# A diffusion layer with a mixture of experts: the order of the work between the router and the first expert

## The chip, the cores and the metric

The kernel runs on one core of one Trainium2 chip. The metric is the device time of one execution in microseconds (us); three runs before gave 1791.06, 1791.74 and 1792.96, median 1791.74. A core has the matrix engine (TensorE, PE in the profile; PEld is its loading of stationary operands), VectorE (DVE), ScalarE (ACT), GpSimd (POOL) and SyncE (SP), which issues most DMAs. Each engine works its own queue in order; semaphores tie the queues together.

## The reference

One layer over 512 latent tokens of width 1024, with 256 context tokens beside them, all in 32-bit floats. First comes a mixer: modulation, a combined projection, a bidirectional state-space scan and a pooling branch, and an output projection. After it come the residual and the part that the change touches, a mixture of 32 experts of which each token takes 4:

```python
x = x + g1 * mixer_out(...)
h = modulate(rmsnorm(x, norm2_w), sh2, sc2)
logits = h @ router_w + router_b
top_val, top_idx = lax.top_k(logits, 4); gates = softmax(top_val)
# for each expert e, over the tokens that chose it:
hb  = h[toks] @ w1[e] + b1[e]              # 1024 -> 2048
g   = minimum(hb[..., ::2], 7); u = clip(hb[..., 1::2], -7, 7)
y   = (g * sigmoid(1.702 * g) * (u + 1)) @ w2[e] + b2[e]     # 1024 -> 1024
out[toks] += gate * y
x = rmsnorm(x + g2 * out, final_norm_w)
```

All 32 experts are computed, so all their weights, 12 MiB for each expert, are read once.

## The kernel before

The program is written for a framework with a planner: the source gives the instructions and their data dependences, the planner simulates the engines and writes each engine's queue in the order in which its simulation starts them. `after(i, j, NoSync)` is an edge that only fixes an order within one engine; `tc.issue_after(j)` gives such an edge to every instruction in its block that runs on j's engine. Instructions that the planner finds ready early can be queued far ahead of their place in the source.

Matrix products keep 32-bit precision by parts: a weight piece of 128 x 2048 (1 MiB, `raw`) is rounded by ScalarE to `hi` (L1093), VectorE takes the remainder `lo = raw - hi` (L1094), and each product is the sum of hi x xh, hi x xl and lo x xh (`prod`, L1353), where xh and xl are the parts of the token rows. An expert has 8 pieces of w1 and 4 of w2. There are three hi/lo pairs, and 9 raw buffers, to which two more (`pm`) are added at the start of `moe`; they lie where the router's small tiles (`pd`) lay. SP loads a piece as soon as its buffer is free (`ring_load`, L1081).

The tokens are four chunks c of 128. For chunk pairs (0, 1) and (2, 3) the output projection ends, then for each chunk `route` (square and norm, eight transposes into `h2t`, the scores by `rw` at L915, top 4, mask), `normed` (the modulated rows `h2`, stored to `h2_scr`, and the residual stored to `acc_scr`) and `table` follow. `table` ranks the tokens of each expert by a product with a triangular matrix (L968) and makes `hot0`, a 0/1 matrix that places the tokens of expert 0. `picked(j, c)` (L1004) multiplies `h2` by it: the token rows of expert 0 are gathered by TensorE, half j of the width in PSUM bank `rows0_[j]`, summed over the chunks. Before, chunks 0, 1 and 2 are picked in `table(2)` and chunk 3 in `table(3)`. `slots` fills the table of tokens and gates for the other experts.

`lead_in` is the turn. It rounds and subtracts the first three weight pieces, and between them in the source stand `in_parts` (the picked rows to xh by ScalarE, L1161, and xl by VectorE, L1162), the gather of the rows of expert 1 from `h2_scr`, and `slots` of chunks 2 and 3. `first` is the last hot matrix of chunk 3 (L977): the first `lo` comes after it on VectorE, and the later loads and the last two stores to `acc_scr` wait for it.

`moe` goes through the experts: w1 of expert p, then w2 of expert p - 1. Expert 16 has two blocks of rows. Two planning steps hang in the product loop: `order()` behind the fourth piece of expert 0 (the order of the remaining experts by their counts) and `beyond()` behind the fourth piece of expert 1 (what exceeds the planned capacities). Both use `Arena` scratch in buffers of the pool `phx`: `order` in `ah`, which before held the residual rows of chunk 3 (x13), and `beyond` in the two `y` buffers (x10 and x11, over which `normed` wrote the `h2` of chunks 2 and 3). The buffer `al` held `sh2`, one of the modulation rows.

Of the kernel before, what the change touches and what calls it, by code (L numbers as in the profile page):

```python
# [16 lines left out]
P = 128  # L17
D = 1024
KT = D // P
# [78 lines left out]
def mixer_and_moe(tc, a):  # L98
# [797 lines left out]
    tops = {}  # L896

    def route(c):
# [15 lines left out]
        for k in range(KT):  # L914
            PE.matmul(lg[:, 0:E], lhsT=h2t[:, k, :], rhs=rw[:, k, :], start=(k == 0), stop=(k == KT - 1))  # L915
# [48 lines left out]
    def table(c):  # L964
# [3 lines left out]
        PE.matmul(rk[:, 0:E], lhsT=c_("up"), rhs=mask[:, c, :], start=(c == 0), stop=True)  # L968
# [15 lines left out]
        if c == 2:  # L984
            rows0_.extend(bank("A") for _ in range(2))
            for j in range(2):
                picked(j, 0)
                picked(j, 1)
                picked(j, 2)
            return  # L990
# [10 lines left out]
    def picked(j, c):  # L1001
        for i in range(4):
            k = 4 * j + i
            PE.matmul(rows0_[j][:, i * P:(i + 1) * P], lhsT=h2s[c][:, k * P:(k + 1) * P], rhs=hot0[c],  # L1004
                      start=(c == 0 and i == 0), stop=(c == NT - 1), skip_group_check=True)
# [56 lines left out]
    newest_lo = [None]  # L1062
# [25 lines left out]
    def ring_split(r):  # L1088
        pool, th, tl, n = hring[turn[1] % len(hring)]
        hi = pool.tile([P, W], F32R, name="hi", tag=th, bufs=n)  # L1090
        lo = pool.tile([P, W], F32R, name="lo", tag=tl, bufs=n)
        turn[1] += 1
        ia = SC.activation(hi, r, AF.Copy)  # L1093
        i = VE.tensor_tensor(lo, r, hi.bitcast(F32), op=ALU.subtract)  # L1094
        newest_lo[0] = i
        if 0 < loads[0] <= LEAD:
            after(ia, last_act[0], mybir.DependencyClass.NoSync, "after the router")
            after(i, first[0], mybir.DependencyClass.NoSync, "after the first slots")
        return hi, lo
# [55 lines left out]
    def in_parts(banks):  # L1155
        hi = pc.tile([P, KT, P], F32R, name="xh", tag="xh", bufs=1)
        lo = pc.tile([P, KT, P], F32R, name="xl", tag="xl", bufs=1)
        for h, bk in enumerate(banks):
            o = hi[:, h * 4:(h + 1) * 4, :]
            v = bk.rearrange("p (k t) -> p k t", k=4)  # L1160
            SC.activation(o, v, AF.Copy)  # L1161
            i = VE.tensor_tensor(lo[:, h * 4:(h + 1) * 4, :], v, o.bitcast(F32), op=ALU.subtract)  # L1162
        return (hi, lo), i
# [8 lines left out]
    def lead_in():  # L1172
        first_ = None
        for i in range(LEAD):
            lead.append(ring_split(ring_load(w1_piece(0, i))))
            if first_ is not None:
                after(newest_lo[0], first_, mybir.DependencyClass.NoSync, "by turns")
            if i == 1:
                after(newest_lo[0], xl_, mybir.DependencyClass.NoSync, "the first rows go ahead")
            if i == 0:  # L1180
                parts0, xl_ = in_parts(rows0_)
# [13 lines left out]
    for pr in range(2):  # L1195
# [7 lines left out]
        for c in cs_:  # L1203
# [6 lines left out]
              lead, slt, sel2)  # L1210
# [45 lines left out]
def moe(tc, a, c_, cst, psa, psb, phx, pc, pd, g2, b1h, b2h, msum, top4, tab, last, table_out, acc_scr, halfneg,  # L1256
        ring, raw, load, split, w1_piece, w1_pair, w2_pair, gather_, transposed_, xgs, lead, slt, sel2):
# [158 lines left out]
    class Arena:  # L1416

        def __init__(self, tags=(("ah", 1), ("al", 1))):
# [154 lines left out]
    for p in range(E):  # L1573
        e = ids[p] = expert(p)
        m = CAPS[p][0]
        if p != MID:
# [3 lines left out]
            for k in range(KT):  # L1580
# [14 lines left out]
                if p == 1 and k == BEYOND_AT:  # L1595
                    beyond()
# [214 lines left out]
```

## Time and profile before

| what | value |
|---|---|
| median of three runs | 1791.74 us (1791.06 to 1792.96) |
| the profiled execution | 1794.53 us, span 1792.7 us |
| mean granted TensorE clock | 0.966 |
| busy share of the span | PE 92%, DVE 85%, ACT 65%, POOL 33% |
| DMA | 521 MB, 291 GB/s over the span |

The span runs from the first to the last instruction; the execution's own time is 1.8 us more. Output projection and router end at about 585 us, expert 0 begins at 590.77 us, and the experts go on until about 1770 us. In timelines a row has start, duration, engine, line, operation, what it writes and reads, shapes, and how many instructions are merged (xN); a 32-bit matrix product stands as two records. In brackets stands the time for which the engine sat idle before the row, and what ended it. A clock of 1.00 is 2.4 GHz, 0.50 is 1.2 GHz.

### The profile page before, as it was taken

To read this page: it belongs to the slowest core of one execution; us is meant where nothing else is said; L and a number is where in the kernel's file an instruction comes from. 1 tells how busy PE (TensorE), PEld (TensorE's weight loads), DVE (VectorE), ACT (ScalarE), POOL (GpSimd) and SP (SyncE) were. 2 spreads that over 40 slices of the span, in tenths; PEclk is the share of its full clock that TensorE was granted. 3 is DMA by queue.
4 is the path that set the end of the run, shared out by engine and by line. 5 is a ranking of instruction groups with operands and counts; after the bars stand their busy time and mean duration, and the time that the engine had idled before them with its cause. 6 is when DMAs were issued, how large, how long until landed. Compare 5 with 4: busy or idle time off the path is not lost. (4 is left out here: it accounts for less than half of the span.)

```text
span 1792.7 us, 21257 instructions
## 1 busy us (share of the span) xinstructions
PE 1640.6 (92%) x7311; PEld 1203.0 (67%) x7311; DVE 1526.3 (85%) x1486; ACT 1170.2 (65%) x1207; POOL 596.2 (33%) x287
## 2 busy tenths in 40 slices
PE   6999889998899899999999999999999998999985
PEld 2777667776778677767766667766666666666653
DVE  7768888987777899899999999976799999999993
ACT  6445436556643577687777777755678787777772
POOL 1203456779210011152041440502063362322302
PEclk9989999999999899999999999999999999999996
DMA  9646443223568789999999999976899999999952
GB/s 352 198 126 214 152 153 114 92 83 113 194 221 325 290 329 365 377 380 382 377 370 379 377 381 390 353 298 202 339 370 388 388 365 372 384 373 377 382 207 103
DMA packets 138417, 521.44 MB, mean 291 GB/s; under 512 B 14798, under 2 KB 44942, under 8 KB 106560
## 3 DMA queue, kind: packets, MB, share of 16 engines
q1 hardware_dynamic: 125446, 490.39, 72.1%
q0 software_dynamic: 6736, 16.70, 4.0%
q10 hardware_dynamic: 6122, 12.94, 2.2%
q8 instruction: 59, 0.97, 0.2%
q14 instruction: 54, 0.44, 0.1%
HBM read 508.26 MB, written 18.37 MB: 294 GB/s over the span
## 5 line engine op out<-in xcount | busy, mean ns | idle before, releaser
L1094 DVE TENSOR_TENSOR lo<-raw,hi 128x2048 fp32r<-128x2048 f32 x398 | 896.9, 2283 | 88.8 <-ACT hi L1093 86.2
L1093 ACT ACTIVATE hi<-raw 128x2048 fp32r<-128x2048 f32 x398 | 751.8, 1915 | 183.8 <-PE A L1353 112.8
L1376 POOL DMA_INDIRECT acc_scr<-y,ixi x32 | 220.7, 6896 | 549.4 <-DVE y L1374 445.3
L1353 PE MATMUL A<-lo,xh 128*128 128x512 f32 (+3 forms) x1072 | 314.0, 410 | 32.6 <-DVE lo L1094 28.7
L1353 PE MATMUL A<-hi,xh 128*128 128x512 f32 (+3 forms) x1072 | 308.5, 404 | 11.5 <-ACT hi L1093 6.9
L1353 PEld LDWEIGHTS A<-lo,xh 128*128 128x128 f32 (+3 forms) x1072 | 187.1, 183 | 120.7 <-DVE lo L1094 72.1
L1353 PEld LDWEIGHTS A<-hi,xh 128*128 128x128 f32 (+3 forms) x1072 | 193.9, 184 | 69.7 <-ACT hi L1093 9.6
L1117 POOL DMA_INDIRECT xg<-h_scr,ixi x30 | 114.3, 3810 | 259.6 <-PE S L1127 175.3
L1353 PE MATMUL S<-lo,ah 128*128 128x512 f32 (+3 forms) x512 | 165.3, 404 | 15.2 <-DVE lo L1094 15.1
L1353 PE MATMUL S<-hi,ah 128*128 128x512 f32 (+3 forms) x512 | 164.6, 402 | 3.9 <-DVE ah L1130 3.9
L1353 PE MATMUL A<-hi,xl 128*128 128x512 f32 (+3 forms) x544 | 155.7, 399 | 0.0
L1353 PEld LDWEIGHTS S<-lo,ah 128*128 128x128 f32 (+3 forms) x512 | 90.3, 183 | 49.9 <-DVE lo L1094 24.3
L1353 PEld LDWEIGHTS A<-hi,xl 128*128 128x128 f32 (+3 forms) x544 | 96.0, 177 | 32.1
L1353 PEld LDWEIGHTS S<-hi,ah 128*128 128x128 f32 (+3 forms) x512 | 92.5, 184 | 33.8 <-DVE ah L1130 4.0
L228 ACT ACTIVATE hi<-raw 128x1024 fp32r<-128x1024 f32 (+1 forms) x73 | 75.9, 1045 | 38.8 <-PE A L355 13.4
L231 DVE TENSOR_TENSOR lo<-raw,hi 128x1024 fp32r<-128x1024 f32 (+1 forms) x59 | 77.1, 1311 | 17.7 <-ACT hi L228 17.0
L1353 PE MATMUL S<-hi,al 128*128 128x512 f32 (+3 forms) x272 | 85.6, 396 | 0.0
L630 ACT ACTIVATE row<-row,nb 128x128 f32<-128x128 f32 x192 | 59.5, 390 | 37.4 <-POOL row L626 37.4
L336 PE MATMUL A<-hx,hi 128*128 128x512 f32 x160 | 66.5, 416 | 3.5 <-DVE at L378 2.1
L338 PE MATMUL A<-hx,lo 128*128 128x512 f32 x160 | 66.4, 415 | 0.0
L337 PE MATMUL A<-hx,hi 128*128 128x512 f32 x160 | 65.6, 410 | 0.0
L378 DVE SCALAR_TENSOR_TENSOR at<-A,cw,at 128x510 f32<-128x510 f32 (+1 forms) x80 | 57.9, 740 | 7.2 <-ACT at L374 6.6
(464 smaller groups left out, 2457.9 us busy)
## 6 DMA issues: line engine op xcount, KB each, us to landing
raw<-in_w_dram SPq DMA_DIRECT2D x384, 1024.0 KB
raw<-in_w_in_dram SPq DMA_DIRECT2D x36, 512.0 KB
mraw<-in_w_mod_dram SPq DMA_DIRECT2D x32, 512.0 KB
raw<-in_w_out_dram SPq DMA_DIRECT2D x14, 1024.0 KB
row<-cs_scr ACTq DMA_DIRECT2D x32, 384.0 KB
raw<-in_w_mod_dram SPq DMA_DIRECT2D x16, 512.0 KB
raw<-in_w_in_dram SPq DMA_DIRECT2D x16, 384.0 KB
xt<-in_x_dram SPq DMA_DIRECT2D x4, 512.0 KB
```

The source lines that it names most:

```text
L228: SC.activation(hi, r, AF.Copy)
L231: e.tensor_tensor(lo, r, hi.bitcast(F32), op=ALU.subtract)
L336: PE.matmul(lat, lhsT=hi[:, k, :], rhs=row_of(hxh, k), start=(k == 0), stop=False)
L337: PE.matmul(lat, lhsT=hi[:, k, :], rhs=row_of(hxl, k), start=False, stop=False)
L338: newest[0] = PE.matmul(lat, lhsT=lo[:, k, :], rhs=row_of(hxh, k), start=False, stop=(k == KT - 1))
L378: VE.scalar_tensor_tensor(ac[:, u:v], src[:, u + o:v + o], cw[:, j, ct:ct + 1], ac[:, u:v], op0=ALU.mult, op1=ALU.add)
L630: SC.activation(row[:, h, :], row[:, h, :], AF.Exp, bias=nb[:, c, i:i + 1])
L1093: ia = SC.activation(hi, r, AF.Copy)
L1094: i = VE.tensor_tensor(lo, r, hi.bitcast(F32), op=ALU.subtract)
L1117: PO.indirect_dma_start(out=t[0:m, :], out_offset=None, in_=h2_scr, in_offset=bass.IndirectOffsetOnAxis(ap=col[0:m, :], axis=0), bounds_ch ...
L1353: PE.matmul(bk[0:n, :], lhsT=u[:, k, 0:n], rhs=v[:, j * 512:(j + 1) * 512], start=(k == 0 and i == 0), stop=((last or m == LT and k == KT ...
L1376: PO.indirect_dma_start(out=acc_scr, out_offset=bass.IndirectOffsetOnAxis(ap=icol[0:m, :], axis=0), in_=y[0:m, :], in_offset=None, bounds_ ...
```

## The change

`picked` takes an instruction to come after on TensorE. The picks of chunks 0 and 1 move from `table(2)` into `table(3)`, where each follows the last score product of chunk 3; the picks of chunk 2 follow the rank product of chunk 3. In `lead_in` the third weight's rounding comes after the roundings of the picked rows on ScalarE. `Arena` takes `al` first and `ah` second. All VectorE instructions of `beyond` come after the subtraction of expert 1's fourth weight piece.

```diff
--- before.py
+++ after.py
@@ -894,6 +894,7 @@
     last_act = [None]
 
     tops = {}
+    scores = {}
 
     def route(c):
         junk = xgs[c % 2]
@@ -912,7 +913,8 @@
                 VE.tensor_copy(o, tp)
         lg = bank("S")
         for k in range(KT):
-            PE.matmul(lg[:, 0:E], lhsT=h2t[:, k, :], rhs=rw[:, k, :], start=(k == 0), stop=(k == KT - 1))
+            x = PE.matmul(lg[:, 0:E], lhsT=h2t[:, k, :], rhs=rw[:, k, :], start=(k == 0), stop=(k == KT - 1))
+        scores[c] = x
         lgs = pd.tile([P, E], F32, name="lgs", bufs=2)
         VE.scalar_tensor_tensor(lgs, lg[:, 0:E], r2s[:, c:c + 1], rbb, op0=ALU.mult, op1=ALU.add)
         top = pd.tile([P, 8], F32, name="top", bufs=2)
@@ -965,7 +967,14 @@
         rk = bank("S")
         if c:
             PE.matmul(rk[:, 0:E], lhsT=c_("ones"), rhs=msum[:, c - 1, :], start=True, stop=False)
-        PE.matmul(rk[:, 0:E], lhsT=c_("up"), rhs=mask[:, c, :], start=(c == 0), stop=True)
+        if c == NT - 1:
+            for i in range(2):
+                for j in range(2):
+                    picked(j, i, scores[c])
+        x = PE.matmul(rk[:, 0:E], lhsT=c_("up"), rhs=mask[:, c, :], start=(c == 0), stop=True)
+        if c == NT - 1:
+            for j in range(2):
+                picked(j, 2, x)
         VE.tensor_tensor(rkm[:, c, :], rk[:, 0:E], mask[:, c, :], op=ALU.mult)
         if c:
             VE.tensor_tensor(msum[:, c, :], msum[:, c - 1, :], mask[:, c, :], op=ALU.add)
@@ -983,10 +992,6 @@
             return
         if c == 2:
             rows0_.extend(bank("A") for _ in range(2))
-            for j in range(2):
-                picked(j, 0)
-                picked(j, 1)
-                picked(j, 2)
             return
         for j in range(2):
             picked(j, c)
@@ -998,11 +1003,13 @@
 
     hot0, rows0_ = [], []
 
-    def picked(j, c):
+    def picked(j, c, then=None):
         for i in range(4):
             k = 4 * j + i
-            PE.matmul(rows0_[j][:, i * P:(i + 1) * P], lhsT=h2s[c][:, k * P:(k + 1) * P], rhs=hot0[c],
-                      start=(c == 0 and i == 0), stop=(c == NT - 1), skip_group_check=True)
+            x = PE.matmul(rows0_[j][:, i * P:(i + 1) * P], lhsT=h2s[c][:, k * P:(k + 1) * P], rhs=hot0[c],
+                          start=(c == 0 and i == 0), stop=(c == NT - 1), skip_group_check=True)
+            if then is not None:
+                after(x, then, mybir.DependencyClass.NoSync, "the router goes ahead")
 
     def slots(c, then=None):
 
@@ -1059,7 +1066,7 @@
 
     W = 2 * FF
     turn = [0, 0]
-    newest_lo = [None]
+    newest_hi, newest_lo = [None], [None]
     loads = [0]
     own = [(strm, SR)]
     ring = [(pcat, RC)] * 3 + [(strm, SR)] * SR + [(pcat, RC)] * (RC - 3)
@@ -1092,7 +1099,7 @@
         turn[1] += 1
         ia = SC.activation(hi, r, AF.Copy)
         i = VE.tensor_tensor(lo, r, hi.bitcast(F32), op=ALU.subtract)
-        newest_lo[0] = i
+        newest_hi[0], newest_lo[0] = ia, i
         if 0 < loads[0] <= LEAD:
             after(ia, last_act[0], mybir.DependencyClass.NoSync, "after the router")
             after(i, first[0], mybir.DependencyClass.NoSync, "after the first slots")
@@ -1158,9 +1165,9 @@
         for h, bk in enumerate(banks):
             o = hi[:, h * 4:(h + 1) * 4, :]
             v = bk.rearrange("p (k t) -> p k t", k=4)
-            SC.activation(o, v, AF.Copy)
+            x = SC.activation(o, v, AF.Copy)
             i = VE.tensor_tensor(lo[:, h * 4:(h + 1) * 4, :], v, o.bitcast(F32), op=ALU.subtract)
-        return (hi, lo), i
+        return (hi, lo), x, i
 
 
     xgs = [pc.tile([P, D], F32, name=f"xg{i}") for i in range(2)]
@@ -1175,10 +1182,12 @@
             lead.append(ring_split(ring_load(w1_piece(0, i))))
             if first_ is not None:
                 after(newest_lo[0], first_, mybir.DependencyClass.NoSync, "by turns")
+            if i == 2:
+                after(newest_hi[0], xh_, mybir.DependencyClass.NoSync, "the first rows go ahead")
             if i == 1:
                 after(newest_lo[0], xl_, mybir.DependencyClass.NoSync, "the first rows go ahead")
             if i == 0:
-                parts0, xl_ = in_parts(rows0_)
+                parts0, xh_, xl_ = in_parts(rows0_)
                 ts = pc.tile([P, 1, 3], F32, name="fts")
                 VE.tensor_copy(ts, tab[:, FT:FT + 3].rearrange("p (e s) -> p e s", s=3))
                 ix = slot_tokens(ts, 1, pc, "f")
@@ -1207,7 +1216,7 @@
 
     psa = moe(tc, a, c_, cst, psa, psb, phx, pc, pd, g2, b1h, b2h, msum[:, NT - 1, :], top4, tab, first[0], table_out,
               acc_scr, halfneg, ring, ring_raw, ring_load, ring_split, w1_piece, w1_pair, w2_pair, gather, transposed, xgs,
-              lead, slt, sel2)
+              lead, slt, sel2, newest_lo)
     pc.release()
     phx.release()
     pcat.release()
@@ -1254,7 +1263,7 @@
 
 
 def moe(tc, a, c_, cst, psa, psb, phx, pc, pd, g2, b1h, b2h, msum, top4, tab, last, table_out, acc_scr, halfneg,
-        ring, raw, load, split, w1_piece, w1_pair, w2_pair, gather_, transposed_, xgs, lead, slt, sel2):
+        ring, raw, load, split, w1_piece, w1_pair, w2_pair, gather_, transposed_, xgs, lead, slt, sel2, newest_lo):
     nc = tc.nc
     SC, VE, PO, PE, SP = nc.scalar, nc.vector, nc.gpsimd, nc.tensor, nc.sync
     ident = c_("ident")
@@ -1415,7 +1424,7 @@
 
     class Arena:
 
-        def __init__(self, tags=(("ah", 1), ("al", 1))):
+        def __init__(self, tags=(("al", 1), ("ah", 1))):
             self.spaces = [phx.tile([P, KT * P], F32, name="arena", tag=t, bufs=b) for t, b in tags]
             self.at = 0
 
@@ -1593,7 +1602,8 @@
                 if p == 0 and k == ORDER_AT:
                     order()
                 if p == 1 and k == BEYOND_AT:
-                    beyond()
+                    with tc.issue_after(newest_lo[0].ins):
+                        beyond()
             sl = selector(p)
             act = phx.tile([P, FF], F32, name="act", bufs=1)
 
```

## Rows read from the trace of the kernel before

**Rows 1.** Stretches of 40 us: from:to, its length, then busy us and instructions of PE, PEld, DVE, ACT and POOL, the granted clock, the DMA engines' share and GB/s. The first is of the steady part, the second of expert 16.

```profile
670.00:710.00 40.00, 40.00 (x186) 31.51 (x185) 37.59 (x27) 30.42 (x20) 6.78 (x4) 1.00 0.98 371
...
1190.00:1230.00 40.00, 37.10 (x165) 28.41 (x164) 19.42 (x15) 18.02 (x15) 2.69 (x2) 0.91 0.38 139
```

**Rows 2.** Who waited for whom on ScalarE from 665 to 1790 us: us in total, times, longest.

```profile
ACT hi L1093 <- PE A L1353: 97.3, 90, 4.1
...
ACT hi L1093 <- DMA raw<-in_w_dram: 2.9, 1, 2.9
```

**Rows 3.** TensorE's timeline at the turn (L1004 picks, L915 scores, L968 ranks, L1353 expert products).

```profile
571.98 2.62 PE L1004 MATMUL A<-hot,h 128*128 128x128 f32 x22
574.44 1.87 PE L915 MATMUL S<-rw,h2t 128*128 128x32 f32 x16
...
576.37 1.36 PE L1004 MATMUL A<-hot,h 128*128 128x128 f32 x10
...
578.91 1.97 PE L915 MATMUL S<-rw,h2t 128*128 128x32 f32 x16 [0.31 <-ACT h2t L910]
...
582.12 3.54 PE L1004 MATMUL A<-hot,x 128*128 128x128 f32 x16 [0.79 <-DVE hot L975]
...
585.52 0.39 PE L968 MATMUL S<-mask,con 128*128 128x32 f32 x2
...
586.54 2.05 PE L1004 MATMUL A<-hot,x 128*128 128x128 f32 x16 [0.25 <-DVE hot L975]
...
590.77 0.74 PE L1353 MATMUL A<-hi,xh 128*128 128x512 f32 x2 [2.18 <-DVE ixa L1186]
...
593.25 1.19 PE L1353 MATMUL A<-hi,xh 128*128 128x512 f32 x2 [0.63 <-DVE xl L1162]
```

**Rows 4.** ScalarE's timeline at the turn.

```profile
571.80 1.09 ACT L910 ACTIVATE h2t<-S 128x512 f32<-128x512 f32 x2 [3.02 <-PE S L907]
574.20 1.06 ACT L900 ACTIVATE xg<-x 128x1024 f32<-128x1024 f32 x1 [1.30 <-DVE x L1202]
...
582.82 5.50 ACT L1093 ACTIVATE hi<-raw 128x2048 fp32r<-128x2048 f32 x3
588.21 1.06 ACT L1161 ACTIVATE xh<-A 128x512 fp32r<-128x512 f32 x2
```

**Rows 5.** VectorE's timeline at the turn.

```profile
581.29 0.24 DVE L917 SCALAR_TENSOR_TENSOR lgs<-S,r2s,rbb 128x32 f32<-128x32 f32 x1
...
583.02 0.36 DVE L932 TENSOR_REDUCE mask<-oh 128x32 f32<-128x128 f32 x1
...
585.70 0.16 DVE L1446 CAST arena<-con 128x1 bf16<-128x1 f32 x1 [1.56 <-PE S L978]
...
586.59 2.29 DVE L1094 TENSOR_TENSOR lo<-raw,hi 128x2048 fp32r<-128x2048 f32 x1
...
590.03 0.68 DVE L1162 TENSOR_TENSOR xl<-A,xh 128x512 fp32r<-128x512 f32 x1
...
592.32 0.18 DVE L1483 SCALAR_TENSOR_TENSOR arena<-cnt,con 32x32 f32<-32x32 f32 x1 [1.55 <-DMA acc_scr<-x]
592.43 0.67 DVE L1162 TENSOR_TENSOR xl<-A,xh 128x512 fp32r<-128x512 f32 x1
593.03 2.27 DVE L1094 TENSOR_TENSOR lo<-raw,hi 128x2048 fp32r<-128x2048 f32 x1
```

**Rows 6.** The turn cut where the granted clock changes; columns as in the first group.

```profile
578.44:581.85 3.41, 2.58 (x22) 2.31 (x20) 3.24 (x19) 1.18 (x4) 1.20 (x1) 1.00 0.48 190
581.85:585.27 3.42, 3.15 (x15) 3.15 (x15) 2.18 (x15) 2.75 (x4) 0.00 (x0) 0.50 0.00 0
585.27:592.09 6.82, 4.39 (x33) 3.81 (x32) 4.97 (x25) 4.00 (x4) 0.42 (x1) 1.00 0.69 239
592.09:598.92 6.83, 6.20 (x15) 4.47 (x14) 6.60 (x11) 1.91 (x1) 0.83 (x1) 0.50 0.66 235
```

**Rows 7.** SP's queue: the first weight load issued after the nine early ones, and a group of three in the first expert.

```profile
588.90 0.44 SPq L1081 DMA_DIRECT2D raw<-in_w_dram  x1
...
616.93 1.35 SPq L1081 DMA_DIRECT2D raw<-in_w_dram  x3
```

**Rows 8.** TensorE's timeline in the second expert.

```profile
629.01 1.57 PE L1353 MATMUL A<-hi,xh 128*128 128x512 f32 x4 [2.80 <-ACT hi L1093]
...
642.40 1.10 PE L1353 MATMUL A<-lo,xh 128*128 128x512 f32 x4
...
645.16 1.07 PE L1353 MATMUL A<-lo,xh 128*128 128x512 f32 x4
```

**Rows 9.** VectorE's timeline in the first expert (slots of chunk 3 among the weights) and in the second.

```profile
599.55 0.29 DVE L1012 TENSOR_TENSOR rkk<-oh,rkm 128x128 f32<-128x128 f32 x1
...
599.90 2.27 DVE L1094 TENSOR_TENSOR lo<-raw,hi 128x2048 fp32r<-128x2048 f32 x1
602.10 0.27 DVE L1015 TENSOR_REDUCE topr<-rkk 128x4 f32<-128x128 f32 x1
...
631.47 0.40 DVE L1556 TENSOR_SCALAR arena<-con,arena 128x48 f32<-128x48 f32 x2
...
638.77 2.28 DVE L1094 TENSOR_TENSOR lo<-raw,hi 128x2048 fp32r<-128x2048 f32 x1
...
642.47 2.28 DVE L1094 TENSOR_TENSOR lo<-raw,hi 128x2048 fp32r<-128x2048 f32 x1
```

## The prediction

> **What bounds the kernel now.** I read the stages first, then who waits for whom in the expert part, then the engines' timelines at the turn (571 to 600 us), then the stretches by clock, then SP's queue and the second expert. All times are us from the span's start.
>
> In a typical 40 us of the expert part TensorE is busy throughout, VectorE 94% and the DMA engines 98% [rows 1]: three candidates. The waits separate them. From 665 to 1790 ScalarE's rounding of a weight piece waited 97.3 us for TensorE and only 2.9 us for a load [rows 2], and at 1190 to 1230 the loads pause (DMA share 0.38) while TensorE goes on at 37.1 of 40 [rows 1]. So the weights lie ready, and the part is paced by the loop of rounding, subtraction and product. A microsecond won or lost before that loop is running should therefore arrive at the end nearly whole; how much of the turn's time is won is the question.
>
> At the turn the end of one long chain starts the experts: scores of the last chunk (578.91 to 580.88), its mask (until 583.38), its rank product (585.52), the products that pick its rows (586.54 to 588.59), their rounding (588.21 to 589.27), the subtractions `xl` (590.03 and 592.43), first expert products at 590.77 and 593.25 [rows 3 to 5]. Each of the two expert starts comes 0.06 and 0.15 us after the end of an `xl` subtraction (590.03 + 0.68 and 592.43 + 0.67), so I read `xl`, which frees the PSUM banks, as their gate, whatever name the bracket has.
>
> **Part 1: the picking products behind the scores.** Removed from in front of the scores: 22 records, 2.62 us, and 10 records, 1.36 us [rows 3]. Chunk 2's scores can then follow its last copy, which ends at 571.80 + 1.09 = 572.89 [rows 4]; 16 records of 1.87 us in two halves end about 574.3 instead of 576.31. Then come chunk 3's transposes, its square on ScalarE (from 574.20, 1.06 plus a 0.18 readout), its two copies (1.09) to about 576.4, and its scores to about 577.9. Before: 580.88. That is 3.0 us earlier.
>
> The 32 records now run there: 32 x 2.62/22 = 3.8 us, to 581.7. Meanwhile VectorE makes the mask; from the start of `lgs` to the mask's end it took 583.38 - 581.29 = 2.1 us [rows 5], so it is ready near 580.0 and hidden under the picks, with 1.7 us to spare. The rank product then starts at 581.7 rather than 585.52, because chunk 2's picks (3.54 us) no longer stand before it. They move behind it and cover the 1.0 us in which VectorE makes the hot matrix (585.52 to 586.54). The remaining 32 records take 3.8 us from 582.1: end at 585.9, against 588.59.
>
> The clock is this part's uncertainty. Before, TensorE was granted 0.50 (1.2 of 2.4 GHz) from 581.85 on, after a stretch of 2.58 busy out of 3.41 us, most of it narrow products [rows 6], and 16 picks took 3.54 us instead of 1.9 [rows 3]. The same narrow work and its waits now lie before the first picks. A fall there costs 15 records x (0.221 - 0.119) = 1.6 us. So this part is worth 2.7 us without a fall and 1.1 with one; the ends are equally near, I take 1.9.
>
> **Part 2: the copies ahead of the third weights, scratch elsewhere.** From the end of the picks to the second expert start passed 593.25 - 588.59 = 4.66 us. Two things go. VectorE waited 1.55 us, with the second `xl` behind it in its queue, until chunk 3's rows were stored in acc_scr [rows 5]: `order`'s scratch overwrote x13, and in `al` it overwrites sh2, whose last reader is chunk 3's normalization, long done. And `beyond`'s small instructions leave this place (the first is at 585.70, itself a 1.56 us wait [rows 5]; that one hid behind the picks of chunk 2, but would no longer). ScalarE rounds three weights in a row before the rows, 582.82 to 588.32 [rows 4]; with the rows earlier than that it would be the next gate, and the new edge puts the third behind them. That third weight then ends some 2.5 us after the picks, and its products come after those of two whole weights: covered.
>
> Now: first half rounded about 0.4 us before the picks end, `xl` 0.65, start 0.3 us after the picks; the first 6 products 1.85 us; second start 2.15 us after the picks. 4.66 - 2.15 = 2.5 us. With part 1 that is 4.4 us for TensorE. A second half-speed stretch, 592.09 to 598.92, came after 4.39 busy of 6.82 us [rows 6]. Its idle pieces (2.18, 0.63 [rows 3]) shrink to some 0.3; if it does not come, TensorE wins up to 3.4 us more.
>
> That last gain can't all be kept. VectorE's second weight subtraction (593.03) follows the second `xl`, so it moves by 4.2 to 5.8 us, and VectorE is nearly full behind it; it frees the buffers for the loads. SP's queue is in order. After nine early loads the next goes out at 588.90, right after the first subtraction (586.59 + 2.29); that one follows the hot matrix and so moves 2.2 to 3.8 us. The last two of the group at 616.93 go behind a load that waits for a subtraction [rows 7], and for one of these TensorE waits until 629.01 [rows 8]. So I credit the turn with what VectorE and the loads allow: 5.5 us, bounds 2.2 (the first load's least) and 7.8 (4.4 + 3.4).
>
> **Part 3: `beyond` behind the second expert's fourth subtraction.** It is the cost. 45 of its VectorE instructions, 6.2 us together, ran from 585.70 to 631.87, partly in time when VectorE waited anyway (the first and the last of them in [rows 5, 9]). All go behind the subtraction that ended at 638.7 (or earlier by the shift), in front of the next ones at 638.77 and 642.47. Those end at 641.05 and 644.75, and TensorE uses them at 642.40 and 645.16: slack 1.4 and 0.4 us [rows 8, 9]. Queued behind are the weight subtractions, and TensorE waits for those. Bounds: 0, if the planner spreads them, and 6.2 - 0.4 = 5.8 if they go in one block. The order shown when a weight is ready is nearer to spreading: `rkk` at 599.55, a whole weight at 599.90, and only then its dependent reduction at 602.10 [rows 9]. `beyond` is mostly such a chain; only its first, independent instructions (casts, fills, differences, some 2.2 us by my count of their 0.06 to 0.2 us each) come at once. Less 1.4 of slack: 0.8 us. `beyond`'s few products on TensorE carry no edge; they follow their inputs. No step moves a DMA in SP's queue: the two last stores to acc_scr still wait for the hot matrix, go ahead of the first late load as before, and shift with it.
>
> **Sum.** -5.5 + 0.8 = -4.7 us. The profiled execution took 1794.53 (span 1792.7), so 1789.8; the median of the runs is 2.79 below that execution, so 1787.0 there. This kernel can be told from no change to about 0.2%, 3.6 us: 1788.2 to 1795.3 is "same".
>
> **The rivals.**
>
> *VectorE becomes the late one in the second expert (slower).* The 6.2 us go in one block: TensorE stalls 5.8 us at the products of 642, and like the idle time before 590.77 this one is followed by half speed, 3.4 to 6.8 us of it [rows 6], costing 1.7 to 3.4. With the turn's 5.5: +2 to +3.7, and with a turn of only 2.2, +5.3 to +7. Taken together 1796. It decides from about 5 us of `beyond` in front of the product at 645. For it: the slack of 0.4 [rows 8, 9]. Against it: the order shown in rows 9. 18%.
>
> *The weights' stream is the bound.* If the DMA share near 1 meant that, only the first late load's shift would count (2.2 to 3.8 us), `beyond` would cost nothing, and the time would be 1791.74 - 3.0 = 1788.7. For it rows 1, against it rows 2. 10%. The Trainium skill's "SBUF — State Buffer", section "A bandwidth-pool intuition that's wrong (but worth ruling out)", speaks for it: "HBM is almost always your end-to-end bottleneck". By that rule the sum would be this rival's; the 2.9 us of waits for loads speak against the rule here.
>
> *The late loads take it back.* If the last two of rows 7 don't move, since their buffers lie on the router's pool and wait for its last readers, TensorE starts the next expert earlier and waits longer, to 629 as now: 0 to -1, plus 0.8, so 1791.5. 17%.
>
> *More than forecast.* The clock stays up at both places and the stall before 629.01 shrinks by its 2.8 us: -7.8 - 2.8 + 0.8 = -9.8, 1782. 10%.
>
> *The forecast*, 1787.0, own range 1784 to 1789.5: 45%, three quarters of it beyond the 0.2%.
>
> **The numbers.** Faster: 0.34 + 0.10 = 0.44. Same: 0.11 + 0.10 + 0.17 + 0.02 = 0.40. Slower: 0.16. The range 1781 to 1795 leaves out the far half of the slower rival and a little of the largest gain, together under 0.2.
>
> **What would show it.** Right, if chunk 3's scores end near 578 and the last picks between 585.5 and 588 (relative to an output projection ending at 571.1), if VectorE no longer waits for acc_scr, and if the second expert start is about 2 us behind the last pick. The third part is right if the subtractions after the fourth of the second expert are spaced 2.3 to 3 us; gaps of 5 us and TensorE waiting there show the first rival. The second expert's second product at 629 or later, with the first expert finished earlier, shows the third rival. I am wrong if the expert part itself, from the third expert on, changes its pace, or if the planner orders the turn in another way than the edges say.

## The result and the profile after

The changed kernel took 1801.97 us (1797.74 to 1808.51, 6 runs), the kernel before 1792.35 beside it (1788.91 to 1794.93, 6 runs): a ratio of 1.0052, interval 1.0038 to 1.0066. That is 9 us slower, where I had forecast 4.7 us faster. The profiled execution of the changed kernel took 1801.61 us.

| | before | after |
|---|---|---|
| span | 1792.7 us | 1799.8 us |
| mean granted clock | 0.966 | 0.971 |
| output projection ends | 571.27 | 572.40 |
| first expert product, behind that | 19.50 | 15.98 |
| ScalarE's rounding for TensorE, 665 to 1790 | 97.3 us | 90.0 us |

In this table the turn is won, the clock is better, and yet the span is 7.1 us longer. TensorE's timeline at the turn after the change, in the same columns as [rows 3]:

```profile
577.01 1.08 PE L916 MATMUL S<-rw,h2t 128*128 128x32 f32 x8 [0.23 <-ACT h2t L911]
...
578.15 1.06 PE L916 MATMUL S<-rw,h2t 128*128 128x32 f32 x8
579.04 2.03 PE L1009 MATMUL A<-hot,h 128*128 128x128 f32 x16
...
583.03 0.40 PE L974 MATMUL S<-mask,con 128*128 128x32 f32 x2
583.26 2.03 PE L1009 MATMUL A<-hot,x 128*128 128x128 f32 x16
...
586.54 1.14 PE L1009 MATMUL A<-hot,x 128*128 128x128 f32 x8
588.38 0.73 PE L1362 MATMUL A<-hi,xh 128*128 128x512 f32 x2 [0.70 <-DVE xl L1169]
...
589.89 0.63 PE L1362 MATMUL A<-hi,xh 128*128 128x512 f32 x2
...
597.73 0.98 PE L1144 MATMUL S<-con,xg 128*128 128x128 f32 x7 [1.62 <-DMA xg<-h_scr,ixa]
```

The scores of chunk 3 (the last row of L916) stand ahead of every pick (L1009), the rank product at 583.03 follows the first two groups, and no row is stretched by a slow clock. Counted from the end of the output projection, the last picks end 15.28 us behind it (before 17.32) and the second expert start stands 17.49 us behind it (before 21.98). In the last row the transposes of expert 1's rows wait 1.62 us for their gather, which nothing waited for before. VectorE and ScalarE there, as in [rows 4, 5]:

```profile
584.65 2.29 DVE L1101 TENSOR_TENSOR lo<-raw,hi 128x2048 fp32r<-128x2048 f32 x1
...
587.66 0.67 DVE L1169 TENSOR_TENSOR xl<-A,xh 128x512 fp32r<-128x512 f32 x1
...
588.62 0.67 DVE L1169 TENSOR_TENSOR xl<-A,xh 128x512 fp32r<-128x512 f32 x1
```

```profile
582.39 3.70 ACT L1100 ACTIVATE hi<-raw 128x2048 fp32r<-128x2048 f32 x2
586.72 0.60 ACT L1168 ACTIVATE xh<-A 128x512 fp32r<-128x512 f32 x1 [0.63 <-PE S L987]
587.72 0.60 ACT L1168 ACTIVATE xh<-A 128x512 fp32r<-128x512 f32 x1 [0.41 <-PE A L1009]
588.21 1.91 ACT L1100 ACTIVATE hi<-raw 128x2048 fp32r<-128x2048 f32 x1
```

Two roundings of weights, then the rows' copies, then the third rounding; the two `xl` follow each other with no wait for acc_scr. Now the second expert, which answers to [rows 8], on TensorE (the last row lies in the third expert):

```profile
624.71 1.61 PE L1362 MATMUL A<-hi,xh 128*128 128x512 f32 x4 [2.67 <-ACT hi L1100]
...
638.02 1.20 PE L1362 MATMUL A<-lo,xh 128*128 128x512 f32 x4 [0.48 <-DVE lo L1101]
...
647.39 0.74 PE L1346 MATMUL A<-b1h,sel 64*128 64x512 f32 x4
657.16 0.27 PE L1472 MATMUL S<-arena 128*128 128x6 bf16 x4 [9.02 <-DVE arena L1464]
...
657.71 1.20 PE L1362 MATMUL S<-hi,ah 128*128 128x512 f32 x2
...
662.92 0.62 PE L1362 MATMUL S<-hi,ah 128*128 128x512 f32 x2
...
729.24 0.73 PE L1362 MATMUL S<-lo,ah 128*128 128x512 f32 x2 [1.01 <-DVE lo L1101]
```

At 624.71 the kernel is 4.3 us ahead of before (629.01 [rows 8]). The bias of expert 1 ends its first projection, and then TensorE does nothing for 9.02 us: the next entry of its queue is a product of `beyond` (L1472, 0.27 us of work), which waits for a VectorE result of L1464. Behind it stand the products of the first expert's second projection, whose first weight piece was rounded and subtracted by 648.74. After the wait their rows of two records follow each other at some 0.86 us until 662.92, and then at 0.46. The same product as in the last row, with the same 1.00 us wait, stood 7.8 us earlier in the kernel before:

```profile
721.42 0.92 PE L1353 MATMUL S<-lo,ah 128*128 128x512 f32 x2 [1.00 <-DVE lo L1094]
```

So the lead of 4.3 us has become an arrears of 7.8, and the span ends 7.1 longer. What TensorE waited for is in VectorE's timeline:

```profile
633.29 0.23 DVE L1450 SCALAR_TENSOR_TENSOR arena<-tope,perm,topr 128x16 f32<-128x16 f32 x1
...
635.22 0.16 DVE L1451 TENSOR_REDUCE arena<-arena 128x4 f32<-128x16 f32 x1
...
638.22 2.28 DVE L1101 TENSOR_TENSOR lo<-raw,hi 128x2048 fp32r<-128x2048 f32 x1
640.42 0.22 DVE L1450 SCALAR_TENSOR_TENSOR arena<-tope,perm,topg 128x16 f32<-128x16 f32 x1
...
640.70 2.28 DVE L1101 TENSOR_TENSOR lo<-raw,hi 128x2048 fp32r<-128x2048 f32 x1
...
645.61 0.15 DVE L1451 TENSOR_REDUCE arena<-arena 128x4 f32<-128x16 f32 x1
...
651.20 0.16 DVE L1460 CAST arena<-arena 128x4 bf16<-128x4 f32 x1
651.27 2.27 DVE L1101 TENSOR_TENSOR lo<-raw,hi 128x2048 fp32r<-128x2048 f32 x1
...
654.34 0.15 DVE L1461 TENSOR_TENSOR arena<-arena 128x4 f32<-128x4 f32 x1
...
655.45 0.15 DVE L1462 CAST arena<-arena 128x4 bf16<-128x4 f32 x1
...
656.27 0.15 DVE L1463 TENSOR_TENSOR arena<-arena 128x4 f32<-128x4 f32 x1
...
656.94 0.15 DVE L1464 CAST arena<-arena 128x4 bf16<-128x4 f32 x1
```

Its nine rows of L1450, L1451 and L1460 to L1464 are one chain: each needs the one before it (the second L1450 overwrites the tile that the first L1451 reads). Each link takes some 0.15 to 0.2 us, but between most of them stand weight subtractions of 2.28 us or pieces of the activation. The chain therefore takes from 633.29 to 657.09, though VectorE is not held up by it. Only behind it may the product run. The stretches around the wait, columns as in [rows 1]:

```profile
647.39:652.60 5.21, 0.74 (x5) 0.30 (x4) 5.21 (x7) 2.06 (x3) 0.00 (x0) 1.00 0.99 376
652.60:662.80 10.20, 5.64 (x18) 4.58 (x19) 5.62 (x24) 0.44 (x1) 0.00 (x0) 0.50 0.63 233
```

The granted clock is 0.50 (1.2 GHz) for 10.2 us. TensorE had been idle since 648.13 when it fell, and was idle in the first 4.6 us of it. And ScalarE, whose three hi/lo pairs were all taken, stood still with it:

```profile
662.36 1.91 ACT L1100 ACTIVATE hi<-raw 128x2048 fp32r<-128x2048 f32 x1 [12.91 <-PE S L1362]
```

### The profile page after: what moved, and what is told of

It reads as the page before. It is cut to its first block, busy times and chain, and to the rows that moved or that the text cites. A ratio compares the mean times of both kernels' runs of the same rounds, so it can differ in the third digit from the quotient of the medians.

```text
span 1799.8 us, 21253 instructions
## 1 busy us (share of the span) xinstructions
PE 1635.6 (91%) x7311; PEld 1195.0 (66%) x7311; DVE 1525.9 (85%) x1486; ACT 1170.8 (65%) x1207; POOL 618.6 (34%) x287
## 5 line engine op out<-in xcount | busy, mean ns | idle before, releaser
L1385 POOL DMA_INDIRECT acc_scr<-y,ixi x32 | 242.6, 7582 | 563.5 <-DVE y L1383 450.3
```

Source lines behind the costliest of these rows:

```text
L1385: PO.indirect_dma_start(out=acc_scr, out_offset=bass.IndirectOffsetOnAxis(ap=icol[0:m, :], axis=0), in_=y[0:m, :], in_offset=None, bounds_ ...
```

## The experiments

The leading theory (A) was: the loss is the wait in TensorE's queue together with the half speed after it, and the turn's gain stays. Its rivals: (B) the turn wins nothing that lasts; (C) `beyond`'s early instructions hold up VectorE at the turn, so that the edge is useful there; (D) the 6.2 us of VectorE work are the cost. Ratios are to runs of the kernel before on the same chip; 0.001 is 1.8 us.

**One part of the change undone or done alone: the edge.** The changed kernel without `beyond`'s edge:

```diff
-                    with tc.issue_after(newest_lo[0].ins):
-                        beyond()
+                    beyond()
```

> The changed kernel without the edge that puts beyond's VectorE instructions behind the second expert's fourth subtraction; the rest of the change stays. Theory A (the loss is made in the second expert, where TensorE waits 9.0 us in its queue for the last VectorE instruction of beyond and then runs 10.2 us at half clock): the turn's gain of some 5 us is left, 4 to 6 us faster than before, so near 1787. Theory B (the reordered turn wins nothing that lasts): between 1 us faster and 1 us slower than before. Theory C (beyond's first instructions, now early again, hold VectorE up in front of chunk 3's hot matrix): 1 to 3 us of the gain are lost again, 1 to 4 us faster than before.

Measured: 1790.8 us, ratio 0.9983 (0.9969 to 0.9997). That is 3.0 us faster (0.5 to 5.6): the sign of A, but short of its 4 to 6, and by the number alone C would do as well. And the kernel before with only these two lines added:

> The kernel before with only the edge on beyond. Theory A: the wait and the half clock come alone, 10 to 15 us slower than before, with TensorE idle for about 9 us in front of beyond's product. Theory B (the loss comes from the turn's new order together with the edge): 0 to 4 us slower, no such wait.

Measured: 1804.63 us, ratio 1.0057 (1.0041 to 1.0073). The place in TensorE's timeline, first without the edge, then with the edge alone:

```profile
649.90 0.73 PE L1346 MATMUL A<-b1h,sel 64*128 64x512 f32 x4
650.56 0.46 PE L1567 MATMUL S<-arena,con 128*128 128x96 f32 x2
650.81 0.70 PE L1362 MATMUL S<-hi,ah 128*128 128x512 f32 x2
```

```profile
654.78 0.74 PE L1337 MATMUL A<-b1h,sel 64*128 64x512 f32 x4
664.55 0.27 PE L1463 MATMUL S<-arena 128*128 128x6 bf16 x4 [9.03 <-DVE arena L1455]
...
665.10 1.20 PE L1353 MATMUL S<-hi,ah 128*128 128x512 f32 x2
```

The wait comes with the edge, 9.03 us to 9.02, whatever the turn looks like, and goes with it. Undoing it moves the ratio from 1.0052 to 0.9983, 12.4 us. The trace's own sum is 9.02 + 2.5 = 11.5: from 657.71 to 662.92 six rows take 5.21 us, and at 0.46 each six take 2.76. Theory B falls as the source of the loss, since the second run has the loss and the wait without the turn's new order; that the turn wins little is not excluded, for the first run's interval reaches into B's band of 1 us. Theory C falls by two traces whose turn ran at full clock: with the edge the last picks end 15.28 us behind the output projection and the first expert product comes 15.98 behind it; without it (the last run of this section) the picks end at 15.28 too, and the product comes at 16.10. The edge is worth 0.1 us there, not 1 to 3.

**The same VectorE order, the products elsewhere.** The edge stays, but `beyond`'s two groups of products are put behind the first expert's second projection in TensorE's queue:

```diff
-    def extra_out(o1, R1, bank_, pool, pre):
+    def extra_out(o1, R1, bank_, pool, pre, then=None):
         for c in range(NT):
-            PE.matmul(bank_[:, 0:6], lhsT=o1[:, c, :], rhs=R1[:, c, 0, :], start=(c == 0), stop=(c == NT - 1))
+            x = PE.matmul(bank_[:, 0:6], lhsT=o1[:, c, :], rhs=R1[:, c, 0, :], start=(c == 0), stop=(c == NT - 1))
+            if then is not None:
+                after(x, then, "the second projection goes ahead")
...
                 if pend is not None:
                     end = C(*pend)
+                if p == 1:
+                    beyond_products(newest_mm[0])
```

> The changed kernel with beyond's two groups of products moved in TensorE's queue behind the products of the first expert's second projection; the edge on VectorE stays. Theory A (it is the wait of TensorE's queue on beyond's chain): the 9 us and the half clock go, 3 to 5 us faster than before. Theory D (the 6.2 us of VectorE work between the subtractions cost the time, as the prediction's slower rival had it): TensorE still falls behind at the subtractions, 1 to 6 us slower than before.

Measured: 1792.54 us, ratio 0.9997 (0.9986 to 1.0009). The 6.2 us are behind the same subtraction on VectorE as in the changed kernel, and 10 of the 12.4 us of loss are gone. In TensorE's timeline the second projection now follows the bias of expert 1 with no wait, and `beyond`'s product finds its input ready:

```profile
651.10 0.73 PE L1346 MATMUL A<-b1h,sel 64*128 64x512 f32 x4
651.76 0.72 PE L1364 MATMUL S<-lo,ah 128*128 128x512 f32 x2
...
671.38 0.26 PE L1475 MATMUL S<-arena 128*128 128x6 bf16 x4
```

So it is the place in TensorE's queue that made most of the loss. The time itself, 0.5 us faster than before (2.5 faster to 1.6 slower), lies between the forecasts: A had said 3 to 5 us faster, D 1 to 6 slower. The 0.0014 that the run lacks to the kernel without the edge lie within the intervals; a later run bears on them.

**The edge three weights earlier**, behind the second expert's first subtraction instead of its fourth:

```diff
-                    with tc.issue_after(newest_lo[0].ins):
+                    with tc.issue_after(behind.ins):
                         beyond()
+                if p == 1 and k == 0:
+                    behind = newest_lo[0]
```

> The changed kernel with the edge behind the second expert's first subtraction instead of its fourth, so that beyond's chain has the time in which VectorE waits for late loads. Theory A: the chain is done before TensorE reaches its product, 4 to 6 us faster than before. Theory D: still 6 us of VectorE work more in the second expert, 0 to 4 us slower than before.

Measured: 1793.88 us, ratio 1.0002 (0.9992 to 1.0013). A's 4 to 6 us faster was missed, and the number lies in D's band. The trace says why: the first product of `beyond` finds its chain done and goes at 627.94 without a wait, but the second does not:

```profile
645.13 0.74 PE L1346 MATMUL A<-b1h,sel 64*128 64x512 f32 x4
648.43 0.43 PE L1567 MATMUL S<-arena,con 128*128 128x96 f32 x2 [2.56 <-DVE arena L1565]
```

A wait of 2.56 us in place of 9.02, and a loss over the kernel without the edge of 0.0019 (3.4 us) in place of 12.4: the shorter wait goes with the smaller loss, though the intervals of these two runs overlap.

**The parts of the turn, each alone on the kernel before.** The picks:

```diff
+        if c == NT - 1:
+            for i in range(2):
+                for j in range(2):
+                    picked(j, i, scores[c])
...
-                picked(j, 0)
-                picked(j, 1)
-                picked(j, 2)
```

> The kernel before with part 1 alone: the picks of chunks 0 and 1 behind chunk 3's scores, those of chunk 2 behind its rank product; the scratch and the third weight's rounding stay as before. Theory 'each part pays for itself' (my prediction's sum): the last picks end about 1 to 2.7 us earlier after the end of the output projection than before (17.32 us there: 571.27 to 588.59), and the time falls by 1.1 to 2.7 us. Rival 'one gate behind the other': with the rows ready earlier the rounding of the third weight on ScalarE (its end 588.32 before) and the wait for acc_scr on VectorE (592.43 before) become the gates, so the second product of expert 0 starts within 0.5 us of before, 22 us after the output projection, and the time stays within 0.7 us of before.

Measured: 1792.49 us, 0.9993 (0.9984 to 1.0003). The scratch alone:

```diff
-        def __init__(self, tags=(("ah", 1), ("al", 1))):
+        def __init__(self, tags=(("al", 1), ("ah", 1))):
```

> The kernel before with the scratch alone: the planner of the remaining experts' order takes the buffer of the modulation row first. Theory 'each part pays for itself': VectorE no longer waits 1.55 us for acc_scr between the two subtractions of the picked rows, the second product of expert 0 starts 1 to 1.6 us earlier, and the time falls by 1 to 1.6 us. Rival 'one gate behind the other': the copies of the rows, behind three rounded weights, set the start, the wait goes and the time stays within 0.5 us. Second rival: the early instructions of the order, now ready before the picked rows, stand in front of the subtractions and cost up to 1 us.

Measured: 1794.85 us, 1.0006 (0.9990 to 1.0023). The wait of 1.55 us for acc_scr was gone there, and the second expert start stood 0.8 us nearer to the output projection (21.17 against 21.98). The rounding's edge alone:

```diff
+            if i == 2:
+                after(newest_hi[0], xh_, mybir.DependencyClass.NoSync, "the first rows go ahead")
```

> The kernel before with one edge alone: the third weight's rounding behind those of the picked rows on ScalarE. Before, the three roundings ended at 588.32 and the picks at 588.59, so ScalarE was free when the rows came. Both theories: no gain at the start of expert 0 by itself (0 to 0.3 us); a loss of up to 1 us if the third weight, ready 2.9 us later, is late for its products, which stand about 5 us behind the first product of expert 0.

Measured: 1793.71 us, 1.0003 (0.9993 to 1.0012). And the picks with the scratch, which is the changed kernel without `beyond`'s edge and without the rounding's:

```diff
-            if i == 2:
-                after(newest_hi[0], xh_, mybir.DependencyClass.NoSync, "the first rows go ahead")
```

> The changed kernel without the edge on the plan's second step and without the edge that puts the third weight's rounding behind those of the rows. With the picks earlier (ending near 587.3 in the kernel without the first edge) and three roundings from about 580 to 587, ScalarE is free at about the time when the rows come. If the parts add (picks 0.9993, scratch 1.0006, rounding 1.0003 alone): 0.9995 to 1.0002. If the picks and the free scratch need each other but not the rounding's edge: 0.9980 to 0.9988, as the kernel without the first edge alone. If all three need each other: 0.9993 or more.

Measured: 1793.65 us, 0.9992 (0.9981 to 1.0004). None of the four differs from 1 by more than its interval, and the four intervals overlap. That the three parts together win 3 us (0.9983) is measured; how it divides among them in the time, and whether they need each other, these runs do not settle.

The profiles say more about the turn itself. With the picks alone the last picks end 15.29 us behind the output projection (586.75 - 571.46), as forecast, and the rival's 22 us for the second expert start is refuted. Three profiles without `beyond`'s edge ran from the output projection to the first expert product at full clock, and there the two expert starts stand 16.75 and 18.26 us behind it with the picks alone, 16.75 and 18.25 with picks and scratch, and 16.10 and 17.61 with all three parts (the last run of this section). So behind the picks the scratch wins nothing at this place, since the second `xl` stands ahead of the wait for acc_scr there, and the rounding's edge wins 0.65 us. The stretches with the picks alone and with picks and scratch, columns as in [rows 1]:

```profile
571.46:588.21 16.75, 14.75 (x127) 13.87 (x124) 15.38 (x65) 10.24 (x15) 3.30 (x3) 1.00 0.67 254
```

```profile
573.50:590.25 16.75, 14.74 (x127) 13.87 (x125) 15.54 (x68) 10.24 (x15) 3.30 (x3) 1.00 0.67 250
```

**The new wait for the gather.** Without the edge, expert 1's transposes waited 2.11 us for their rows. I put them behind the products of expert 0's fourth piece:

```diff
+                if p == 0 and k == 3:
+                    with tc.issue_after(newest_mm[0].ins):
+                        nxt = next_x(1)
-                if k == 2:
+                if p and k == 2:
                     nxt = next_x(p + 1)
```

> The changed kernel without the edge on the plan's second step, and the transposes of expert 1's rows behind the products of expert 0's fourth piece. In the changed kernel TensorE waited 1.62 us for the gather of these rows, without the edge 2.11 us. Theory 'what TensorE wins in front of the steady loop stays': the wait goes, no other takes its place, and the time is 1.5 to 2.5 us below the changed kernel without the edge (1790.8), so 1788 to 1789.5, ratio to before 0.996 to 0.9975. Rival 'the loads and subtractions decide': TensorE waits as much longer for the roundings at the end of expert 0 (2.96 us there without the edge), and the time is that of the changed kernel without the edge within 0.5 us.

Measured: 1795.59 us, 1.0013 (1.0001 to 1.0024): neither forecast holds. The wait for the gather is gone, but in the planner's new order TensorE again waits for `beyond`'s second product ahead of the second projection:

```profile
654.57 0.74 PE L1346 MATMUL A<-b1h,sel 64*128 64x512 f32 x4
657.82 0.43 PE L1570 MATMUL S<-arena,con 128*128 128x96 f32 x2 [2.51 <-DVE arena L1568]
```

So I combined this with the later products (`beyond_products(newest_mm[0])` behind `end = C(*pend)`, as above):

> The kernel with expert 1's transposes later and no edge on the plan's second step (1795.59, ratio 1.0013), and that step's two groups of products on TensorE behind the second projection of expert 0. In the profile of that kernel TensorE waited 2.51 us in the second expert for the second product of the step. Theory 'the queue of TensorE': that wait was the loss; it goes, no other of over 1 us stands in the second expert, and the time falls by 2.5 to 4 us, to a ratio between 0.9985 and 1.000. Rival 'the later transposes themselves cost' (rows of expert 1 late for its first product, or weights held longer): the time stays within 1 us of 1795.59, ratio 1.001 to 1.002.

Measured: 1791.76 us, 0.9988 (0.9975 to 1.0002), with no wait of over 0.7 us left in the second expert behind its second piece. Against the run before, that is 0.0025 or 4.5 us for a wait of 2.51, theory A's direction, though the intervals (1.0001 to 1.0024, 0.9975 to 1.0002) still touch. Without the wait for the gather it is no faster than the kernel that has it (0.9988 against 0.9983). The same later products on the kernel without the edge, the transposes left where they were:

> The changed kernel without the edge on the plan's second step, and with that step's two groups of products behind the second projection of expert 0. Without the edge TensorE had no wait for the step, so theory 'the queue of TensorE' says: as the kernel without the edge (ratio 0.9983), within 1.5 us of it, 0.9975 to 0.9992. Rival: moving the products costs something by itself (the step's results come later, TensorE's and VectorE's order shifts), as the run with the edge kept and the products later (0.9997) may mean: 0.9993 or more.

Measured: 1792.47 us, 0.9995 (0.9985 to 1.0005), just on the rival's side, though its interval holds both. Whether moving the products costs something is open. Against the 0.9997 with the edge kept it shows that the edge, once TensorE doesn't wait behind it, costs nothing that can be measured: theory D is left with what the two intervals, some 2 us to either side each, can hide. Last, the transposes behind the third piece instead of the fourth (against the first kernel of this part):

```diff
-                if p == 0 and k == 3:
+                if p == 0 and k == 2:
```

> The changed kernel without the edge on the plan's second step, with the transposes of expert 1's rows behind the products of expert 0's third piece (one piece earlier than in the run before, 4 products later than without any such edge). Theory 'what TensorE wins in front of the steady loop stays': the wait for the gather, 2.11 us without it, falls to under 0.7 us, the step's products wait nowhere, and the time is 1 to 2 us below the kernel without the edge: ratio 0.9972 to 0.9980. Rival 'the loads and subtractions decide': as the kernel without the edge, 0.9980 to 0.9990. If the planner's new order makes TensorE wait over 2 us for the step's products again, 0.9995 or more.

Measured: 1791.38 us, 0.9984 (0.9972 to 0.9995). The wait for the gather shrank as meant, and the next one grew:

```profile
600.51 1.09 PE L1144 MATMUL S<-con,xg 128*128 128x128 f32 x8 [0.48 <-DMA xg<-h_scr,ixa]
...
628.80 2.08 PE L1364 MATMUL A<-hi,xh 128*128 128x512 f32 x4 [4.48 <-ACT hi L1100]
```

0.48 instead of 2.11 us there, but 4.48 instead of 2.96 at the second expert's second piece: what the first stop gave up, the second took. The time is that of the kernel without the edge, as the rival said. These two, the changed kernel without `beyond`'s edge and this one, are faster than both kernels by their intervals: 3 us under the one before and 12 under the changed one. Against the one before it is by little (the intervals end at 0.9997 and 0.9995), and they are the best two of a dozen.

## Why the prediction was wrong

**What failed: part 3**, in its sentence "`beyond`'s few products on TensorE carry no edge; they follow their inputs". They follow their inputs, but in a queue in order, and what stands behind them follows too. I priced the edge by the 6.2 us that it moves on VectorE and by the slack of the weight subtractions, 0.8 us with bounds 0 and 5.8. It cost 12.4 us, and on another engine. The bounds came from a wrong quantity: not how long the chain works, but when its last link ends. A chain of nine links that starts at 633 and gets one link or two between two subtractions of 2.28 us was not done by 648, where TensorE came to its product, and [rows 9] had shown the spreading on which this rests. I took it as good news (VectorE's slack is kept) and did not ask who waits for the end of the chain. The Trainium skill's "TensorE: Matmul & The Clock Gate", section "Step-by-step: what each phase is for", says it of the engine: "The MATMULs themselves stay in program order". The trace agrees: products with ready inputs stood 9.02 us behind one of 0.27 us.

The sign that I named for part 3 was met: the subtractions behind the edge start at 635.74, 638.22, 640.70, 643.41, 646.47, 649.00 and 651.27, spaced 2.3 to 3.1 us, and TensorE waited 0.48 us for one. It looked at VectorE's queue only, where nothing was wrong.

**The first rival** had the sign, the expert and a time of 1796, but the wrong mechanism: `beyond` was not in one block, and with the products moved its work on VectorE cost nothing that can be measured (0.9997 with the edge, 0.9995 without). A wait in TensorE's queue was not among the rivals, and so the range ended at 1795, below the 1802 measured.

**Part 1, the picks**: right by its own signs. Scores of chunk 3 end 6.81 us behind the output projection (forecast 578 - 571.1 = 6.9), last picks 15.28 (forecast 14.4 to 16.9), gain 2.0 there (forecast 1.9). That it hits 1.9 is luck: this was the middle between 2.7 without a fall of the clock and 1.1 with one. The clock did not fall, and against 2.7 the gain is 0.7 too small; the last picks take 4.42 us (583.26 to 587.68) where I had 3.8, with small products of the tables (L987, L1278, L1282) among them that I had left out. With a fall (the kernel without the edge) it was 17.32 - 16.82 = 0.5.

**Part 2**: right by its signs. The wait for acc_scr is gone, and the second expert start stands 589.89 - 587.68 = 2.21 us behind the last pick (forecast 2.15). The reason given for it holds in part only: with the picks alone that distance was already 18.26 - 15.29 = 2.97, and the scratch, credited with the 1.55 us, took nothing from it.

**The turn's sum, 5.5 us, was too large by the medians.** The trace of the changed kernel seemed to confirm it: at the second expert's second piece it is 4.3 us ahead, 5.4 relative to the output projection. But the median without the edge is only 3.0 us under before (interval 0.5 to 5.6, which just holds 5.5). The 5.5 itself was a choice between the bounds 2.2 and 7.8, not a sum. Two terms look mis-sized. First, I credited the absence of the second half-speed stretch to the change, and that differs between executions of the same order (last section). The profiled executions of before and of the kernel without the edge have equal half speed behind the output projection (13.7 us in the 100 us after it, three stretches each); there the first expert product is 19.50 - 17.23 = 2.3 us earlier, and the rest of the span, 1792.7 - 571.27 against 1789.5 - 570.51, is 2.4 us shorter. The two agree with each other and with my lower bound of 2.2, but that the lead passes to the end whole is not shown by them: by the mean clocks (0.966 and 0.969) the kernel before had some 11 us more at 1.2 GHz over the span. Second, TensorE now reaches expert 1's transposes before their rows, a new wait of 1.62 us, and 2.11 without the edge; I had asked what is late next of the weights alone.

**The weights' stream as the bound** fell: 9 us in which TensorE stood still came through to the end, though the DMA engines were still at 0.99 while they began (647.39 to 652.60). The Trainium skill's "SBUF — State Buffer", section "A bandwidth-pool intuition that's wrong (but worth ruling out)", says that HBM, rather than SBUF, is almost always the end-to-end bottleneck; the measurement decides against HBM here.

**The late loads take it back** fell for the changed kernel (624.71 against 629.01, with a wait of 2.67 against 2.80), but a version of it is in the last experiment: a wait of 4.48 us at that place when TensorE came earlier. (Its 1791.5 was the lower end of its own sum, 1791.5 to 1792.5.)

## What to carry to other kernels

When instructions of a chain are moved on one engine, list the products that wait for its last link on every other engine, and read what stands behind these in their queues; the price is the end of the chain against their place, not the chain's work. A small product that belongs to planning should stand behind the work that must not wait for it, by an edge of its own: a change elsewhere can bring it in front again, as the later transposes did. Gains of a few microseconds read from one profile should first be freed of the clock's stretches, which another execution may not have.

## What the runs showed that I had not expected

The clock's falls at the turn are not a property of the queue's order. Three kernels (without the edge, transposes behind the third piece, transposes behind the fourth piece) have the same instructions in the same order on every engine until expert 1's transposes. The stretch from the end of the output projection to the first expert product in each of their profiled executions, columns as in [rows 1]:

```profile
570.51:587.74 17.23, 16.28 (x127) 15.42 (x125) 15.50 (x67) 8.45 (x14) 3.31 (x3) 0.90 0.73 274
```

```profile
574.82:590.92 16.10, 14.74 (x128) 13.87 (x125) 15.29 (x66) 8.86 (x15) 3.29 (x3) 1.00 0.58 213
```

```profile
573.72:593.97 20.25, 19.39 (x127) 18.44 (x125) 15.43 (x67) 8.44 (x14) 2.93 (x3) 0.75 0.53 204
```

The same work took 16.10 us at full clock, 17.23 with 3.4 us at 1.2 GHz, and 20.25 with 10.2 us of it: 4.2 us between executions, nearly the whole of what I had forecast for the change. Each of the three ran on another chip, but the chip is not the reason: two more kernels with this order, on the chip of the 16.10, took 17.35 us with 3.4 at 1.2 GHz and 20.15 with 10.2:

```profile
575.07:595.22 20.15, 19.43 (x127) 18.48 (x125) 15.43 (x67) 8.45 (x14) 2.94 (x3) 0.75 0.55 201
```

What decides it is not shown. The Trainium skill's "TensorE: Matmul & The Clock Gate", section "What's actually happening", calls the number of slow products at a kernel's start run-variable. No run here looks at the start; the traces show the like in the middle of a kernel, with TensorE busy for 19.39 of 20.25 us.

The second is how much one short instruction can hold back: while a product of 0.27 us waited, two engines and the loads stopped or slowed. TensorE waited 9.02 us, ScalarE 12.91, and the DMA engines fell from 0.99 to 0.63.
